# Chunked attention on one core: transposes by 32x32 blocks on VectorE, exchanged through DRAM

## The chip, the cores and the metric

The kernel runs on one core of one Trainium2 chip. The metric is the device time of one execution in microseconds (us); the median of three runs counts. "The profile" is one execution taken by the hardware profiler, and "the page" is its summary.

## What is computed

The reference applies four layers to x, 256 tokens of 1,024 channels, in float32: a gated delta rule, a causal attention of 8 heads, a retention of 4 heads, and a chunked attention of 16 heads of 128 dimensions. Only the last layer changes. Cut to what matters:

```
proj = h @ w_in                       # [256, 8192]
q, k, v, g = split(proj, 4)           # 16 heads of 128 each
q, k = rms_norm(q) * q_g, rms_norm(k) * k_g      # over the 128 of a head
s = q @ k.T / sqrt(128) + bias        # chunks of 64 tokens; what lies ahead of a chunk is masked
o = softmax(s) @ v * silu(g)
x = x + gate * (o @ w_out)            # the output of the kernel
```

## The kernel before

Weights come in units of 128x1024 float32 (512 KB), one DMA each on SyncE's queue into one of five `raw` buffers. ScalarE and VectorE split each unit exactly into two float32r parts, `whi` and `wlo` (`unit`, six pairs of buffers, `PARTS`); activations are kept in two parts as well (`hd_hi`, `hd_lo`), and a product is three products of parts. In layer d, the chunked attention, q, k and v come in quarters of four heads: `project_a` makes two PSUM banks of 128 tokens x 512 columns (two tiles of tokens) out of four units, 96 products of 512 columns. The gates g and the output come as 128 columns x 256 tokens out of one or two units, 24 products of 256 columns a unit (`project_b`).

A quarter of q or k is then normed (`normed`): ScalarE sums squares, GpSimd takes the power, VectorE multiplies PSUM by the factor into `xn` [128 tokens, 4 heads, 128], and four TensorE transposes against the identity (in the trace `con`) put it, head by head, into a PSUM bank. ScalarE copies the bank into `kr`, or reversed in its tokens and scaled into `qr`. A head (`head`, `attend`) waits for its quarters of q, k, v and its bias. Two float32 products give the scores, 384 columns: the first tile of queries with 128 keys, the second with 256. VectorE adds the bias and takes the least, ScalarE takes the exponential and its sum, VectorE divides. Three TensorE transposes turn the weights `s` around, ScalarE copies them from PSUM into `pT`, two products with `vr` give the output, and ScalarE copies that into one of five buffers `or`. A gate (`gate`) multiplies it by silu and splits it for the output projection; only then the buffer `or` comes free. `out_tile` makes 128 output channels at a time, adds them to xT and stores them.

The order of the instructions is written out by a small planner in the kernel (`Tasks`). Tasks are generators that yield operations; the planner gives each operation a time by estimates written in the code and issues per engine in the order in which the engines would take them by these estimates. On the chip each engine runs its instructions in that fixed order and waits on semaphores for the data. A DMA is estimated at 0.05 us and its bytes on the queue, and 2.0 us more until it has landed; a product in float32r at 0.42 ns a column. Priorities let heads go ahead of projections. PSUM has eight banks, in rings that change hands between layers; in layer d before: four for projections (`PJ`), one for scores (`SS`), one for the transposes of weights (`TT`), one for outputs (`OO`), one for the transposes of q and k (`MM`).

The order in which quarters come is a line of letters (line 157), and a head can start as soon as its q, k and v are done:

```
ORDER_D = "q1 k0 v0 q0 v2 g1 q2 k1 v1 q3 v3 g0 g3 k2 k3 g2".split()
```

Here "q1" is the quarter of heads 4 to 7, and the gates of heads 0 to 2 are made ahead, at the end of the layer before. The profile puts nearly all instructions on line 218, the helper that records them, so that groups are told apart by tile names.

Of the kernel before, what the change touches and what calls it, by code (L numbers as in the profile page):

```python
# [10 lines left out]
F32 = mybir.dt.float32  # L11
# [6 lines left out]
PSUM = bass.MemoryType.PSUM  # L18
# [8 lines left out]
# Per-partition columns: (name, number of columns)  # L27
# [12 lines left out]
# Constants that depend on shapes alone: (name, number of columns)  # L40
# [27 lines left out]
def _t5_hot():  # L68
    """[33, 384]: which bucket the relative position 255 - m falls in; the last row masks what lies ahead."""
    rel = 255 - np.arange(384)  # L70
    n = np.maximum(rel, 0)
    nf = np.maximum(n, 1).astype(np.float32)
    large = 16 + (np.log(nf / np.float32(16)) / np.float32(np.log(2048 / 16)) * np.float32(16)).astype(np.int32)
    bucket = np.where(n < 16, n, np.minimum(large, 31))
    hot = np.zeros((33, 384), np.float32)
    hot[bucket, np.arange(384)] = rel >= 0
    hot[32] = np.where(rel >= 0, 0.0, -1e30)
    return hot


def _decay():
    """[128 keys, 4 heads, 384]: key tile 0 with all queries, then key tile 1 with the last 128."""
# [29 lines left out]
def _plan():  # L112
    """The units of weights in the order of their use; those of the adaptive norms stand between the others."""
# [37 lines left out]
# Which units of weights are used whole, in float32 products  # L151
WHOLE = [("d_g", u) for u in (0,)] + [("a_qkv", u) for u in (0, 3, 4, 6, 7, 8, 9, 13, 14, 17, 18, 20, 22)]
# The order of the units
# [3 lines left out]
ORDER_D = "q1 k0 v0 q0 v2 g1 q2 k1 v1 q3 v3 g0 g3 k2 k3 g2".split()  # L157
ADA_FROM = ('a_z', 7)
ADA2_FROM = ('c_v', 3)
# Counts: units used before the norm, steps at once, units ahead, buffers  # L160
EARLY, BATCH, AHEAD, AHEAD2, FIRST_D, ADA_A, ADA2_EVERY = 1, 1, 1, 2, 3, 2, 1
RAWS, NPARTS, NKQ, NC, NVT = 5, 6, 3, 2, 2
# Priorities of tasks, the least goes first
# [4 lines left out]
# Estimates, in us  # L168
OVER, HOP, SAME = 0.03, 0.2, 0.1
DMA_LATENCY = 2.0  # L170
# [10 lines left out]
class Ring:  # L181
    """Free buffers: `b = yield ring` waits for one, ring.put(b) gives one back."""
# [22 lines left out]
class Engine:  # L205
    """Turns the calls of an engine into operations for a task to yield: (engine, estimated us, call, table)."""
# [57 lines left out]
def chain(*ops):  # L264
    """Operations of one engine, each on what the one before it made."""
    return [(e, c + SAME, f, t) for e, c, f, t in ops[:-1]] + [ops[-1]]


class Tasks:
    """Issues the instructions of concurrent tasks in the order in which the engines would take them.  # L270

    A task is a generator. It yields an operation or a list of operations of one engine, and goes on when they have
    ended by the estimates; a Ring, and gets a buffer; an Event, and waits for it; a number, its priority from there on
    (the least goes first)."""
# [59 lines left out]
    def dispatch(self, e):  # L334
# [18 lines left out]
        lat = DMA_LATENCY if e.startswith("D") else 0.0  # L353
# [5 lines left out]
        self.at(end + 1e-6, lambda: self.dispatch(e))  # the next operation of the same task may go first  # L359

    def hold(self, n):
        """While held, the vector and the scalar engine take nothing that can wait."""
        self.held += n
        if not self.held:
            for e in "VS":
                self.at(self.now, lambda e=e: self.dispatch(e))
# [10 lines left out]
def body(ctx, tc, a, out):  # L377
# [4 lines left out]
    dma, dma2 = Engine("D", nc.sync, _cost_dma), Engine("D2", nc.scalar, _cost_dma)  # L382

# [18 lines left out]
    con = tile_(keep, "con", [P, NCON])  # L402
# [9 lines left out]
    nc.scalar.activation(phalf, nhalf, AF.Copy, scale=-1.0)  # the activation table is loaded meanwhile  # L412

    # PSUM: rings of whole banks; they change hands between the layers
# [22 lines left out]
    def h_set(i, name, wide=0):  # L437
        """Two float32r parts of transposed activations."""
# [10 lines left out]
    # ------------------------------------------------------------ weights: units of [128, 1024], in the order of use  # L449
# [11 lines left out]
    def unit(u):  # L461
        """One unit, whole or split exactly into two float32r parts; what belongs to the adaptive norms is summed at once."""
        raw = yield RAW
        src = a[u[0]][u[1]]
        if number[u] == 0:  # its first half is used before the other is there
# [35 lines left out]
    def project_b(units, x, x32, ps, ready):  # L501
        """[128 columns, tokens] of a product. x: (hi, lo) of the transposed activations, x32: the same, not split."""
# [19 lines left out]
    def project_a(name, q, x, pss, ready):  # L522
        """Two [128 tokens, 512 columns] of a product, with four units."""
# [32 lines left out]
    def sums_ops(ps, srcs):  # L556
        """Sums over the partitions of [128, 256] each, tokens on partitions: [128 tokens, 2, 96]."""
# [3 lines left out]
    def row_ops(ps, c):  # L561
        """A pair of token columns along the free dimension, on every partition."""
# [6 lines left out]
    # ------------------------------------------------------------ gated delta rule  # L569
    def layer_a(pool):  # L570
# [44 lines left out]
        def load_consts():  # L615
            yield [dma.dma_start(out=wab, in_=a["a_ab"]), dma.dma_start(out=rows, in_=a["a_rows"].partition_broadcast(P)),
                   dma.dma_start(out=con[:, 2 * P:], in_=a["consts"][:, 2 * P:])] + [
# [9 lines left out]
        def x_square(i):  # L627
            """Squares of two column tiles, added to those before."""
# [30 lines left out]
        def decays():  # L659
            """gg = -exp(a_log) softplus(a + dt_bias), beta = sigmoid(b), tokens on partitions"""  # L660
# [34 lines left out]
        def decay(h):  # L695
            """decay[s, c] = exp(sum of gg over s < m <= c), where the products of queries and keys will stand"""
# [16 lines left out]
        def conv(ch, dst):  # L713
            """dst [128, 256] = silu(conv) of channel tile ch."""
# [36 lines left out]
        def squared(h, x, dst):  # L751
            """Sums of the squares of the columns of x [128, 256]."""
# [7 lines left out]
        def norm_k(h, kq, done):  # L760
            """nk = the norm of the keys, bb = beta / nk ** 2"""
# [14 lines left out]
        def head(h):  # L776
            """The system matrices of head h and its squared norms."""
# [13 lines left out]
            # k.k of key tile 0 (256) and 1 (128), q.k of key tile 0 (256) and 1 (128)  # L791
# [10 lines left out]
            # the 16 x 16 diagonal blocks, side by side; then only what lies between blocks stays in MT  # L802
# [10 lines left out]
        def base(q):  # L813
            """V16 = (I + U)^-1 for the strictly upper 16 x 16 problems of four heads, block rows on partitions."""
# [31 lines left out]
        def gates(q):  # L846
            """zs = silu(z)"""
# [8 lines left out]
        # block solves: (I + B)^-1 = D (I - F)(I + F^2)(I + F^4), F = N D  # L856
# [54 lines left out]
        def outputs(t, q):  # L911
            """The outputs of four heads on one tile of tokens, their norm and gate, transposed in two parts."""
# [68 lines left out]
    def out_a(o_in, z_in, box, after):  # L981
        """The rows of the first four heads for all columns, then those of the others, two column tiles at a time."""
# [7 lines left out]
        # the two column tiles of a bank are one group, begun with zeros  # L990
# [35 lines left out]
    # ------------------------------------------------------------ from one layer to the next  # L1026
    class Next:
        """What the end of a layer makes for the next: scaled activations and sums of squares, a column tile at a time."""
# [24 lines left out]
        def squares(self, n):  # L1053
            """Adds to the sum; works on pairs, but for the last."""
# [22 lines left out]
        def weighted_squares(self, n, w):  # L1077
            """Adds to sums over the channels, tokens on partitions, with one weight of two for each half of the columns."""
# [11 lines left out]
    def ahead(u, nx, box):  # L1090
        """A product begun before its layer is, before norm and shift; box[u] = PSUM, with the product of the shift behind it."""
# [15 lines left out]
    # ------------------------------------------------------------ softmax attention of one head  # L1107
    def attend(A, kT, qT, bias, vv, o, half):
        """o [128 dims, 256] = half times the output; queries stand reversed in their tile of 128 in qT and bias.

        x holds the negative scores, mx their least: minus the maximum of the scores."""
        ps = yield SS
        yield [pe.matmul(ps[:, :P], lhsT=qT[:, :P], rhs=kT[:, :P], start=True, stop=True),
               pe.matmul(ps[:, P:384], lhsT=qT[:, P:], rhs=kT, start=True, stop=True)]
# [11 lines left out]
        ps = yield TT  # L1126
        yield [pe.transpose(ps[:, i * P:(i + 1) * P], x[:, i * P:(i + 1) * P], ident) for i in range(3)]
        A["s"].put(item)
        pT = yield A["pT"]
        yield s.activation(pT, ps[:, :384], AF.Copy)  # L1130
        TT.put(ps)
        ps = yield OO
        yield [pe.matmul(ps[:, :T], lhsT=vv[0], rhs=pT[:, :T], start=True, stop=False),
               pe.matmul(ps[:, P:T], lhsT=vv[1], rhs=pT[:, T:], start=False, stop=True)]
# [10 lines left out]
    def gate_out(o, zs, hi, lo):  # L1145
        """The two parts of o * zs."""
# [4 lines left out]
    # ------------------------------------------------------------ MoBA (one block of 256: causal attention within it)  # L1151
    def layer_b(pool, nx, begun, after):
# [16 lines left out]
        def biases():  # L1169
            """Rows of rel = 255 .. -127 for each head, then [128 - 1 - query, key]."""  # L1170
# [79 lines left out]
        def head(h):  # L1250
# [3 lines left out]
            yield from attend(A, K[h], Q[h], b_bias[:, h], [VV[q][:, t, hh * P:(hh + 1) * P] for t in range(2)], O[h], 1.0)  # L1254
# [43 lines left out]
    # ------------------------------------------------------------ adaptive norms  # L1298
    def cond(condb):
        """condb: silu(c) along the free dimension, on every partition"""  # L1300
# [4 lines left out]
    def ada(i, nx):  # L1305
        """mods[i] [128, 24]: shift, 1 + scale and gate of layer i as columns"""
# [11 lines left out]
    def modulate(hs, i, nx, k, r12, Y, r_in, done):  # L1318
        """hs = parts of rms_norm(x) * norm_g * (1 + scale) + shift"""
# [566 lines left out]
```

## Time and profile before

| what | value |
|---|---|
| three runs, us | 806.8, 804.44, 802.66; median 804.44 |
| span of the profiled execution, first to last instruction | 799.7 us |
| what lies around that span, against the median | 4.7 us |
| TensorE busy in the span | 787.7 us, 98% |
| VectorE, ScalarE, GpSimd busy | 566.3, 456.7, 37.6 us |
| first product of layer d on `hd_hi` | 546.3 us |
| last output product of a head of layer d | 755.7 us |

An engine's busy time counts its instructions from start to end. TensorE's products are pipelined: they start every 0.12 to 0.23 us though each lasts longer, so that the distance between starts says more than the mean of one.

### The profile page before, as it was taken

Reading aid. Unit: us, or ns where it says so; the run is one execution under the profiler, and the core shown is the slowest. Engines: PE = TensorE matmul, PEld = TensorE weight load, DVE = VectorE, ACT = ScalarE, POOL = GpSimd, SP = SyncE. Lnnn points to the kernel's source line nnn. Section 1 sums busy time; section 2 is a strip of 40 time slices with the busy share of each in tenths; the row PEclk is TensorE's granted clock in tenths of the full one; section 3 lists DMA queues with packets and bytes.
Section 4 is the critical chain, followed back from the end, with each engine's and each line's share of the span. In section 5 each row is a group of like instructions: output and inputs, shape, how many; then the busy total and the mean of one; then the engine's idle time right before and its main releaser. Section 6 shows DMA issues by size and latency. Waiting matters only on the chain.

```text
span 799.7 us, 13581 instructions
## 1 busy us (share of the span) xinstructions
PE 787.7 (98%) x5117; PEld 710.3 (89%) x5117; DVE 566.3 (71%) x1157; ACT 456.7 (57%) x968; POOL 37.6 (5%) x45
## 2 busy tenths in 40 slices
PE   6999999999999999999999999999999999999998
PEld 5898889989899999998888879998889888989998
DVE  5799998346997978698467889768547556557751
ACT  4886453545635786644445454655657567558740
POOL 0120100010000000000000000000100000000000
PEclk9999999999999999999999999999999999999999
DMA  8536443125768866728558899865654665564340
GB/s 286 181 106 210 133 143 120 55 80 174 254 219 324 296 218 203 239 77 286 158 142 275 304 309 325 259 185 191 211 177 128 209 181 151 171 187 132 103 132 27
DMA packets 45946, 151.15 MB, mean 189 GB/s; under 512 B 5135, under 2 KB 10040, under 8 KB 45880
## 3 DMA queue, kind: packets, MB, share of 16 engines
q1 hardware_dynamic: 44824, 149.22, 57.9%
q10 hardware_dynamic: 1056, 1.06, 0.5%
q8 instruction: 40, 0.66, 0.3%
q14 instruction: 26, 0.21, 0.1%
HBM read 149.20 MB, written 1.06 MB: 188 GB/s over the span
## 4 chain that ended last, share of the span: by engine, by line
PE 98%; DMA 1%; DVE 0%; ACT 0%; issue 0%; POOL 0%; SPq 0%; DVEq 0%
PE bank L218 98%; DMA xT<-in_xT 1%; ACT js L218 0%; POOL rs L218 0%; DVE r L218 0%; DVE hi L218 0%; ACT r L218 0%; DVE xT L218 0%; DVE lo L218 0%; ACT rsrow L218 0%; SPq L218 0%; DVE rs L218 0%; ACT whi L218 0%; DVEq L218 0%
## 5 line engine op out<-in xcount | busy, mean ns | idle before, releaser
L218 ACT ACTIVATE whi<-raw 128x1024 fp32r<-128x1024 f32 x210 | 222.2, 1060 | 200.8 <-PE bank L218 168.5
L218 DVE TENSOR_TENSOR wlo<-raw,whi 128x1024 fp32r<-128x1024 f32 x210 | 256.0, 1223 | 104.9 <-ACT whi L218 103.8
L218 PE MATMUL bank<-whi,hd_hi 128*128 128x512 f32 x192 | 78.0, 406 | 0.0
L218 PE MATMUL bank<-wlo,hd_hi 128*128 128x512 f32 x192 | 75.7, 394 | 0.0
L218 PE MATMUL bank<-whi,hd_lo 128*128 128x512 f32 x192 | 75.6, 394 | 0.0
L218 DVE CUSTOM_DVE_ANT_0 raw<-raw,condb 128x1024 f32<-128x1024 f32 x48 | 58.5, 1220 | 8.9 <-DMA raw<-in_ada 8.8
L218 PE MATMUL bank<-whi,hc_hi 128*128 128x512 f32 x128 | 52.0, 406 | 0.0
L218 PE MATMUL bank<-whi,hc_lo 128*128 128x512 f32 x128 | 50.5, 395 | 0.0
L218 PE MATMUL bank<-wlo,hc_hi 128*128 128x512 f32 x128 | 50.4, 394 | 0.0
L218 PE MATMUL bank<-lo,raw 128*128 128x256 f32 x192 | 44.3, 379 | 0.9 <-DVE lo L218 0.9
L218 PEld LDWEIGHTS bank<-whi,hd_lo 128*128 128x128 f32 x192 | 36.2, 188 | 8.6
L218 PEld LDWEIGHTS bank<-whi,hd_hi 128*128 128x128 f32 x192 | 36.1, 188 | 7.4
L218 PEld LDWEIGHTS bank<-wlo,hd_hi 128*128 128x128 f32 x192 | 36.2, 188 | 7.4
L218 PEld LDWEIGHTS bank<-lo,raw 128*128 128x128 f32 x192 | 35.1, 189 | 5.4 <-DVE lo L218 1.1
L218 PE MATMUL bank<-hb_hi,whi 128*128 128x256 f32 x128 | 38.4, 300 | 0.0
L218 PE MATMUL bank<-hb_hi,wlo 128*128 128x256 f32 x128 | 36.3, 283 | 0.0
L218 PE MATMUL bank<-hb_lo,whi 128*128 128x256 f32 x128 | 36.1, 282 | 0.0
L218 PE MATMUL bank<-hd_hi,whi 128*128 128x256 f32 x104 | 31.7, 305 | 0.0
L218 PE MATMUL bank<-ha_hi,whi 128*128 128x256 f32 (+1 forms) x96 | 29.5, 307 | 0.0
L218 PE MATMUL bank<-hd_hi,wlo 128*128 128x256 f32 x104 | 29.3, 282 | 0.0
L218 PE MATMUL bank<-hd_lo,whi 128*128 128x256 f32 x104 | 29.3, 282 | 0.0
L218 PEld LDWEIGHTS bank<-whi,hc_lo 128*128 128x128 f32 x128 | 24.1, 188 | 5.7
(322 smaller groups left out, 2157.3 us busy)
## 6 DMA issues: line engine op xcount, KB each, us to landing
raw<-in_ada SPq DMA_DIRECT2D x48, 512.0 KB, 4.6
raw<-in_a_qkv SPq DMA_DIRECT2D x23, 512.0 KB, 4.6
raw<-in_c_v SPq DMA_DIRECT2D x16, 512.0 KB, 4.3
raw<-in_c_g SPq DMA_DIRECT2D x16, 512.0 KB, 4.0
raw<-in_c_out SPq DMA_DIRECT2D x16, 512.0 KB, 4.9
raw<-in_d_g SPq DMA_DIRECT2D x16, 512.0 KB, 3.7
raw<-in_d_q SPq DMA_DIRECT2D x16, 512.0 KB, 3.6
raw<-in_d_k SPq DMA_DIRECT2D x16, 512.0 KB, 3.6
```

The lines of the kernel that those rows point to most:

```text
L218: return self.key, c, lambda: f(*a, **k), func and func.name
```

## The change

In layer d TensorE transposes nothing any more. VectorE transposes each 32x32 block in its place and writes the blocks in an order by which those that belong together lie side by side in a row (`blocks`, `z`). The tile goes out to DRAM in one DMA (`turn_out`), and four DMAs (`turn_in`), each for 32 partitions, read it back so that the row of blocks becomes a column of blocks: with the transposed blocks that is the whole transpose. For a quarter of q or k (128x1024) a piece of these reads is 1,024 bytes long, for a head's weights (128x384) 384 bytes. The reads go into `kr` and `pT` directly; for q they go into a buffer first, from which ScalarE makes `qr`. These DMAs are issued on SyncE's queue, with the weights, and the planner has its own estimate for them: 0.45 us each on the queue and 4.0 us more. Operands of scores and output products are read in runs of 32 elements, because blocks stay interleaved.

Buffers: `z` for q and k is the tile of the silu of c, used no more; a second one and two for the weights come out of the tile x32 as soon as the layer's own activations are made (`more`); a buffer for q is where the constants of the first layer were. The bank of `MM` goes to `PJ`, that of `TT` to `SS`. The quarters come in another order. The other attention (layer b) keeps its transposes on TensorE. Elsewhere the diff takes out comments alone; its core:

```diff
-ORDER_D = "q1 k0 v0 q0 v2 g1 q2 k1 v1 q3 v3 g0 g3 k2 k3 g2".split()
+ORDER_D = "q1 k1 q0 v1 k0 v0 q2 g1 k2 v2 q3 k3 g0 v3 g2 g3".split()
...
-DMA_LATENCY = 2.0
+LATENCY = {"D": 2.0, "D2": 2.0, "DB": 4.0}
...
+    swap = Engine("DB", nc.sync, lambda *x: 0.45)
...
-    con = tile_(keep, "con", [P, NCON])
+    con = tile_(keep, "con", [P, 10 * P])
...
+    def turn_out(z, d):
+        return swap.dma_start(out=d, in_=z)
+    def turn_in(dst, d):
+        w = dst.shape[1] // 4
+        return [swap.dma_start(out=dst[32 * b:32 * b + 32].rearrange("j (a c) -> j a c", c=w),
+                               in_=bass.AP(tensor=d.tensor, offset=d.offset + b * w, ap=[[4 * w, 32], [128 * w, 4], [1, w]]))
+                for b in range(4)]
+    def blocks(x, n):
+        return x.rearrange("p (a m i) -> p m a i", a=4, m=n)
     def attend(A, kT, qT, bias, vv, o, half):
-
-        x holds the negative scores, mx their least: minus the maximum of the scores."""
         ps = yield SS
-        yield [pe.matmul(ps[:, :P], lhsT=qT[:, :P], rhs=kT[:, :P], start=True, stop=True),
-               pe.matmul(ps[:, P:384], lhsT=qT[:, P:], rhs=kT, start=True, stop=True)]
+        yield [pe.matmul(ps[:, :P].rearrange("p (a i) -> p a i", a=4), lhsT=qT[:, 0], rhs=kT[:, 0], start=True, stop=True),
+               pe.matmul(ps[:, P:384].rearrange("p (t a i) -> p t a i", t=2, a=4), lhsT=qT[:, 1], rhs=kT, start=True, stop=True)]
...
-        ps = yield TT
-        yield [pe.transpose(ps[:, i * P:(i + 1) * P], x[:, i * P:(i + 1) * P], ident) for i in range(3)]
-        A["s"].put(item)
-        pT = yield A["pT"]
-        yield s.activation(pT, ps[:, :384], AF.Copy)
-        TT.put(ps)
+        if "z" not in A:
+            ps = yield TT
+            yield [pe.transpose(ps[:, i * P:(i + 1) * P], x[:, i * P:(i + 1) * P], ident) for i in range(3)]
+            A["s"].put(item)
+            pT = yield A["pT"]
+            yield s.activation(pT, ps[:, :384], AF.Copy)
+            TT.put(ps)
+        else:
+            z = yield A["z"]
+            yield v.transpose(blocks(z, 3), x.rearrange("p (m b i) -> p m b i", m=3, b=4))
+            A["s"].put(item)
+            d = tc.dram_tile([P, 384], F32, name="p_d")
+            yield turn_out(z, d)
+            A["z"].put(z)
+            pT = yield A["pT"]
+            yield turn_in(pT, d)
         ps = yield OO
-        yield [pe.matmul(ps[:, :T], lhsT=vv[0], rhs=pT[:, :T], start=True, stop=False),
-               pe.matmul(ps[:, P:T], lhsT=vv[1], rhs=pT[:, T:], start=False, stop=True)]
+        x = blocks(pT, 3) if "z" in A else pT.rearrange("p (m a i) -> p m a i", m=3, a=4)
+        o2 = ps[:, :T].rearrange("p (m a i) -> p m a i", m=2, a=4)
+        yield [pe.matmul(o2, lhsT=vv[0], rhs=x[:, :2], start=True, stop=False),
+               pe.matmul(o2[:, 1], lhsT=vv[1], rhs=x[:, 2], start=False, stop=True)]
...
-        m, rs, r12, qkg = buf("m", [P, 2]), buf("rs", [P, 2]), buf("r12", [P, T]), buf("qkg", [P, 1])
+        A["z"] = Ring(run, [])
+        m, rs, r12, qkg = buf("m", [P, 2]), buf("rs", [P, 2]), acc[:, 0], buf("qkg", [P, 1])
+        ZX, QT = Ring(run, [late["condb"]]), Ring(run, [con[:, 2 * P:]])
         hs = h_set(0, "hd")
         oT = sixteen(pool, "od", nx.hs)
         Y, XN, FR = Ring(run, [r.free[0][:, i] for r in SQ for i in range(2)]), ring(pool, "xn", [P, 4, P], 3), Ring(run, [(buf(f"ms{i}", [P, 2, 4]), buf(f"fr{i}", [P, 2, 4])) for i in range(2)])
-        QR, KR, VR = (ring(pool, n, [P, 4, 2, P], 2) for n in ("qr", "kr", "vr"))
+        QR, KR, VR = (ring(pool, n, x, 2) for n, x in (("qr", [P, 1024]), ("kr", [P, 1024]), ("vr", [P, 4, 2, P])))
...
-            MM.put(ps)
+            PJ.put(ps)
...
-                ps = yield MM
-                yield [pe.transpose(ps[:, hh * P:(hh + 1) * P], xn[:, hh], ident) for hh in range(4)]
+                if t == 0:
+                    z = yield ZX
+                yield v.transpose(blocks(z, 8)[:, 4 * t:4 * t + 4], xn.rearrange("p h (b i) -> p h b i", b=4))
                 XN.put(xn)
-                x = ps.rearrange("p (h i) -> p h i", h=4)
-                if reverse:
-                    yield qkg_in
-                    yield s.activation(dst[:, :, t, ::-1], x, AF.Copy, scale=qkg)
-                else:
-                    yield s.activation(dst[:, :, t], x, AF.Copy)
-                MM.put(ps)
+            d = tc.dram_tile([P, 1024], F32, name=name + "_d")
+            yield turn_out(z, d)
+            ZX.put(z)
+            if reverse:
+                x = yield QT
+                yield turn_in(x, d)
+                yield qkg_in
+                for t in range(2):
+                    yield s.activation(dst[:, t * 512:(t + 1) * 512].rearrange("p (h a i) -> p h a i", h=4, a=4),
+                                       blocks(x, 8)[:, 4 * t:4 * t + 4, ::-1, ::-1], AF.Copy, scale=qkg)
+                QT.put(x)
+            else:
+                yield turn_in(dst, d)
...
-            yield from attend(A, K[q][:, hh].rearrange("p t i -> p (t i)"), Q[q][:, hh].rearrange("p t i -> p (t i)"),
+            yield from attend(A, blocks(K[q], 8)[:, hh::4], Q[q].rearrange("p (t h i) -> p t h i", t=2, h=4)[:, :, hh],
                               B[q][:, hh], [VV[q][:, hh, t] for t in range(2)], o, 0.5)
...
+        def more():
+            for e in hs_in + [first["in", ("d_g", u)] for u in range(FIRST_D)]:
+                yield e
+            x = x32_tile("zd", 2).rearrange("p k t -> p (k t)")
+            for i in range(2):
+                A["z"].put(x[:, 1024 + i * 384:1024 + (i + 1) * 384])
+            ZX.put(x[:, :1024])
+        run.spawn(more(), 1)
...
-        yield from hand_over(OO, TT)
+        yield from hand_over(OO, SS)
```

## Rows read from the trace of the kernel before

**Rows 1.** The page's head: busy time, share of the span, instructions.

```profile
span 799.7 us, 13581 instructions
PE 787.7 (98%) x5117; PEld 710.3 (89%) x5117; DVE 566.3 (71%) x1157; ACT 456.7 (57%) x968; POOL 37.6 (5%) x45
```

**Rows 2.** The chain that ended last, longest piece: start, us, what.

```profile
171.91 624.54 PE bank L218 x4079
```

**Rows 3.** TensorE's groups, 546 to 760 us: busy us, mean ns.

```profile
L218 PE MATMUL bank<-con,xn 128*128 128x128 f32 x64 | 9.6, 273 | 0.0
...
L218 PE MATMUL bank<-con,s 128*128 128x128 f32 x48 | 7.9, 273 | 0.0
```

**Rows 4.** TensorE's timeline at two groups of transposes: start us, us.

```profile
564.58 0.39 PE L218 MATMUL bank<-wlo,hd_hi 128*128 128x512 f32 x1
564.81 0.40 PE L218 MATMUL bank<-whi,hd_lo 128*128 128x512 f32 x1
565.05 0.60 PE L218 MATMUL bank<-con,xn 128*128 128x128 f32 x4
565.41 0.48 PE L218 MATMUL bank<-whi,hd_hi 128*128 128x512 f32 x1
565.73 0.39 PE L218 MATMUL bank<-wlo,hd_hi 128*128 128x512 f32 x1
...
754.20 0.28 PE L218 MATMUL bank<-xd_hi,wlo 128*128 128x256 f32 x1
754.32 0.49 PE L218 MATMUL bank<-con,s 128*128 128x128 f32 x3
754.57 0.36 PE L218 MATMUL bank<-xd_hi,whi 128*128 128x256 f32 x1
754.77 0.28 PE L218 MATMUL bank<-xd_lo,whi 128*128 128x256 f32 x1
754.89 0.28 PE L218 MATMUL bank<-xd_hi,wlo 128*128 128x256 f32 x1
```

**Rows 5.** VectorE's and ScalarE's groups, 546 to 760 us: busy us, mean ns.

```profile
L218 DVE TENSOR_TENSOR wlo<-raw,whi 128x1024 fp32r<-128x1024 f32 x64 | 78.2, 1225 | 61.6 <-ACT whi L218 60.8 <-PE bank L218 0.7
L218 DVE TENSOR_TENSOR xn<-bank,fr 128x512 f32<-128x512 f32 x16 | 10.9, 683 | 0.2 <-POOL fr L218 0.2
...
L218 ACT ACTIVATE pT<-bank 128x384 f32<-128x384 f32 x16 | 7.8, 489 | 1.2 <-PE bank L218 1.1
...
L218 ACT ACTIVATE kr<-bank 128x512 f32<-128x512 f32 x8 | 4.8, 598 | 6.6 <-PE bank L218 6.6
```

**Rows 6.** Stretch of eight heads: busy us of PE, PEld, DVE, ACT, POOL; clock, DMA.

```profile
724.00:757.00 33.00, 33.00 (x254) 31.91 (x253) 24.93 (x85) 26.61 (x84) 1.64 (x1) 1.00 0.35 104
```

**Rows 7.** SyncE's DMA issues, timeline: start us, us of the issue.

```profile
538.12 0.33 SPq L218 DMA_DIRECT2D raw<-in_d_k  x1
538.54 0.39 SPq L218 DMA_DIRECT2D br<-in_d_rel  x1
```

**Rows 8.** SyncE's waits, 546 to 757 us: total us, times, longest.

```profile
SPq L218 <- DVE wlo L218: 132.0, 49, 9.9
```

**Rows 9.** Timeline: the first d_out load, the first d_out product.

```profile
709.83 0.33 SPq L218 DMA_DIRECT2D raw<-in_d_out  x1
...
756.29 0.48 PE L218 MATMUL bank<-od,whi 128*128 128x256 f32 x2
```

**Rows 10.** Issue to landing: eight xT stores of 128 KB; weights from 546 us.

```profile
L218 SPq DMA_DIRECT2D out<-xT x8: 332/338/425, 760.3 to 797.0; - x8
...
DMA to landing us min/median/max: 1.9/2.9/4.7
...
DMA to landing us min/median/max: 3.4/3.6/5.5
```

**Rows 11.** DMA queues: packets, MB, share; 546 to 760 us, then whole span.

```profile
q1 hardware_dynamic: 10272, 34.61, 53.8%
...
q10 hardware_dynamic: 1056, 1.06, 0.5%
```

More of the change, by code (lines that the diff above doesn't have):

```diff
@@ L352, in dispatch @@
         self.free[e] = end
-        lat = DMA_LATENCY if e.startswith("D") else 0.0
+        lat = LATENCY.get(e, 0.0)
         def ended():
@@ L616, in load_consts @@
             yield [dma.dma_start(out=wab, in_=a["a_ab"]), dma.dma_start(out=rows, in_=a["a_rows"].partition_broadcast(P)),
-                   dma.dma_start(out=con[:, 2 * P:], in_=a["consts"][:, 2 * P:])] + [
+                   dma.dma_start(out=con[:, 2 * P:NCON], in_=a["consts"][:, 2 * P:])] + [
                 dma.dma_start(out=V16[q], in_=a["blk_id"]) for q in range(2)]
@@ L1253, in head @@
                 yield e
-            yield from attend(A, K[h], Q[h], b_bias[:, h], [VV[q][:, t, hh * P:(hh + 1) * P] for t in range(2)], O[h], 1.0)
+            yield from attend(A, K[h].rearrange("p (t a i) -> p t a i", t=2, a=4), Q[h].rearrange("p (t i) -> p t i", t=2), b_bias[:, h], [VV[q][:, t, hh * P:(hh + 1) * P] for t in range(2)], O[h], 1.0)
             run.set(o_in[h])
```

## The prediction

> **What bounds the kernel now.** I read the head of the page first. TensorE is busy 98% of the span; the other engines are not near it [rows 1]. A busy TensorE can still hide gaps, so the chain of waits came next: from 171.9 us to the last product, 624.5 us on end, it is TensorE behind TensorE, with no other engine in between [rows 2]. The changed layer (from about 546 us to the end) lies wholly inside. So in this layer one us of TensorE work taken away is one us of time, if what replaces it is never late; and one us for which TensorE waits, its queue being in order, is one us of time, too. Work put on VectorE, ScalarE, SyncE or the DMA engines costs nothing as long as it isn't late.
>
> **What is taken from TensorE.** The changed layer has 64 transposes of xn (16 groups of four: q and k, four quarters, two token tiles) and 48 of s (16 groups of three, one a head) [rows 3]. The row "mean of one", 273 ns, is no price: it is the length of a pipelined instruction. The price is how much later the next products start. One product of 512 columns follows the other in 0.23 us. From the last one ahead of the group of four at 564.81 to the second one behind it at 565.73 are 0.92 us, where two steps without transposes are 0.46: the group costs 0.46 us, the slower restart behind it included [rows 4]. For the group of three: 754.20 to 754.77 are 0.57 us, two steps of 0.12 are 0.24, cost 0.33 us [rows 4]. The sum: 16 x 0.46 + 16 x 0.33 = 7.4 + 5.3 = 12.6 us. Scores and outputs of the heads stay as many and as large. Their operands are read in runs of 32 elements now; no row shows what that costs, the row of the contiguous form gives nothing, and I take nothing; were it a restart of each, it would be at most the 0.1 us by which a product is later behind a group (565.73 - 565.41 = 0.32 against 0.23), twice a head: 32 x 0.1 = 3 us.
>
> **What is moved to VectorE and ScalarE.** VectorE gets 16 transposes of 128x512 and 16 of 128x384. The trace has none of either; the nearest rows are 683 ns for 128x512 with an operand in PSUM and 1225 ns for 128x1024, so 0.6 to 0.7 us for the first; for the second 0.46 (three eighths of 1225) to 0.68 [rows 5]. I take 0.65 and 0.5: 16 x 0.65 + 16 x 0.5 = 18.4 us. ScalarE loses the copies into kr (8 x 0.598) and pT (16 x 0.489), 12.6 us, and keeps those into qr [rows 5]. Where heads stand closest, eight of them between 724 and 757 us, VectorE is busy 24.9 of 33 us [rows 6]; eight more transposes of 0.5 make it 28.9. So VectorE still fits, and the cost on the path is 0. Were it full there, 0.5 us a head would come on top, 16 x 0.5 = 8 us.
>
> **What the exchange costs.** A head's weights go out as one DMA of 192 KB and come back as four of 48 KB, pieces of 384 bytes; a q or k quarter goes out as 512 KB and comes back as four of 128 KB, pieces of 1,024 bytes. That is 24 x 5 = 120 DMAs more on SyncE's queue, 0.33 to 0.39 us each to issue [rows 7]: 40 to 47 us of a queue that between 546 and 757 us waits 132 us for VectorE to free weight buffers [rows 8]. It has room; what it queues is the next weights, and those are far ahead: the first of d_out is issued at 709.8 us and used at 756.3 [rows 9]. So late weights cost 0 unless SyncE lags by tens of us.
>
> The trip itself stands between softmax and output product. Bounds: a 128 KB write lands in 1.9 us at best, 2.9 in the median, a 512 KB load in 3.4 to 5.5 [rows 10]. So out 1.9 to 5.5, three further issues 1.0 to 1.2, the last read 1.9 to 5.5: 4.8 to 12.2 us. I take 3.2 + 1.1 + 3.3 = 7.6, since bytes and crowding lie between the two median rows. The kernel's own plan, which fixes TensorE's order, allows 0.45 + 4.0 out and 4 x 0.45 + 4.0 in: 10.25 us. So at my price data are there 2.6 us before TensorE's turn, and at the upper end 2.0 us after. What covers the trip is projections: after heads 4 to 7 come k0 and v0, after 0 to 3 q2 and g1, after 8 to 11 q3 and k3, after 12 to 15 g2 and g3. Each letter is four units, 4 x 12 x 0.23 = 11 us. Without this cover a trip a group of four heads would be 4 x 7.6 = 30 us. For q and k, the value quarter or another one stands between the projection and its heads, again 11 us or more, so their eight trips are hidden. The reordering does only that: it costs no TensorE work. I add 0.25 us a group (one issue that stands ahead in SyncE's queue is 0.33), 1.0 us.
>
> A weak point is the four reads. The rows show that one queue has several DMAs under way: two issues at 538.12 and 538.54 us, each landing only us later [rows 7, 10], so four reads should overlap. The Trainium skill, "DMA: Bandwidth & Descriptors", section "Rules for kernel authors", speaks against the change: small transfers should be made one large one, as under 64 KB overhead is most of the cost. By the rows' overlap the trip is 7.6 us; by that rule taken as one overhead after the other it becomes the second rival below.
>
> **Sum.** 799.7 us of span [rows 1] - 12.6 + 1.0 = 788.1; the median of the runs shown, 804.44, lies 4.7 us above that span, so the forecast is 792.8 us, 1.4% faster. What a measurement here can tell from no change is about 0.5%, 4 us.
>
> **Rivals.**
> 1. *Trips late by a little.* At the upper bound each group of heads holds TensorE for 2.0 us, 8 us in all: 791.8 + 8 = 799.8 us. For it: DMA engines are 53.8% busy in the layer, and the trips add to that [rows 11]. A packet of 1 KB took 0.5% x 16 x 799.7 / 1056 = 0.06 us; 24 x 512 such pieces and the writes by their bytes (7.3 MB at 53.8% x 16 x 214 / 34.6 = 53 us per MB) are (745 + 390) / 16 = 71 us of all engines in some 200. So it would be near 90% with the longest assumption for the 384-byte pieces. Against it: weights come early and don't press.
> 2. *The four reads of a head one after another.* 3.2 + 4 x 2.9 [rows 10] = 14.8 us, 4.6 late, four groups: 18.2 us, so 791.8 + 18.2 = 810.0 us, slower. It decides from 12.6 / 4 = 3.2 us late a group. Against it: the overlap of issues above. By the page's fixed cost of about 2.0 us a DMA (same page, "Anatomy of one DMA") four reads would be an estimated 8 us and the time about 796; no run so far shows it.
> 3. *The last heads.* Only five output buffers (OR) are there; while heads 8 to 11 wait for their gates in g2, heads 13 to 15 get a buffer only as those gates finish. If head 15's trip begins as late as the end of g3, what covers it is the first d_out tile, 15 steps of three products, 15 x 3 x 0.12 = 5.4 us: TensorE waits 2.2 (trip 7.6) to 6.8 us (12.2), about 4.5: 796.3 us. For it: each gate needs its own unit of 24 x 0.12 = 2.9 us. Against it: g2 and g3 are 23 us long.
> 4. *Weights late.* If SyncE, held by waits for trips, loses the lead of 46 us [rows 9], TensorE waits for weights. The DMA sum above says 90% at most, so a lag of some 10 us would be needed to eat the gain: 802 to 808 us.
>
> **Chances.** Forecast 0.62; first rival 0.13 (0.08 of it over 0.5% faster, 0.05 within); second 0.09, slower; third 0.11, faster; fourth 0.05 (0.03 within, 0.02 slower). Faster 0.62 + 0.08 + 0.11 = 0.81, same 0.08, slower 0.11. The range: from no wait at all, 791.8, less the 1.8 us by which the fastest run lies under the median, 790.0, to the first rival with about 1 us of that spread, 801. It leaves out the second rival and most of the fourth, about 0.14, and a little at either end. The likeliest case alone: 790 to 795.
>
> **What would show it.** Right: transposes of xn gone from TensorE, those of s down to 24 (the other attention's); 32 VectorE transposes of 0.5 to 0.7 us; TensorE's steps in the layer still without a gap; last product near 784.8 us. A trip from VectorE's transpose to the output product's first possible start under 10 us. The first rival: TensorE's waits list DMA into pT, some 2 us a group; the second: the same, over 3 us, and reads that land one by one; the third: one gap of 2 to 7 us between the last gate unit and the first d_out products' end; the fourth: ScalarE's splits wait for weights. Wrong would be the price of the groups if steps between products grew where no wait is shown: then strided operands cost.

## The result

The changed kernel takes 794.35 us (median of 4 runs, 791.45 to 798.13), the kernel before 803.62 us beside it (802.66 to 806.8): a ratio of 0.9884, 95% interval [0.9846, 0.9922]. Forecast were 792.8 us, 790.0 to 801.0. In a second set of runs it was 794.73 us against 802.49, 0.990 [0.9882, 0.9919].

The profiled execution has a span of 792.6 us and a time of 794.41. The head of its page, which answers to [rows 1]:

```profile
span 792.6 us, 13576 instructions
PE 777.4 (98%) x5005; PEld 700.5 (88%) x5005; DVE 581.7 (73%) x1189; ACT 444.4 (56%) x944; POOL 37.4 (5%) x45
```

112 TensorE instructions are gone, VectorE's busy time rose by 15 us, ScalarE's fell by 12. The groups by tile names show what stands in their place: the transposes of the heads (min, median, max in ns), those of the k quarters (the eight of the q quarters, 0.71 us each too, go into `condb`), and what is left of TensorE's transposes of s, all before 294 us and so of the other attention:

```profile
L218 DVE STREAM_TRANSPOSE zd<-s x16: 558/573/579, 599.1 to 736.4; 128x384 f32<-128x384 f32 x16
L218 DVE STREAM_TRANSPOSE zd<-xn x8: 703/705/711, 577.5 to 704.3; 128x512 f32<-128x512 f32 x8
...
L218 PE MATMUL bank<-con,s x24: 270/272/274, 259.6 to 293.2; 128*128 128x128 f32 x24
```

The chain of waits is no longer one piece. TensorE's waits from 540 us on (total, times, longest) are one line, and the chain of waits leads it back through a read and a write of the k3 quarter (start, us, what):

```profile
PE bank L218 <- DMA kr<-d_k_d: 2.5, 1, 2.5
```

```profile
706.06 8.21 DMA d_k_d<-zd
...
715.65 3.73 DMA kr<-d_k_d
719.38 0.14 issue
719.52 69.71 PE bank L218 x557
```

VectorE had finished that quarter at 705.0 us. SyncE issued the write at 706.06, behind four reads of q3 and a load of weights; it landed 8.2 us later, the four reads took 1.3 us to issue, and the last one 3.7 to land. With the 1.05 us ahead of the write that is 14.4 us, where the planner allows 10.25. TensorE's timeline there shows what it cost:

```profile
716.75 0.28 PE L218 MATMUL bank<-hd_hi,wlo 128*128 128x256 f32 x1
719.52 0.89 PE L218 MATMUL bank<-kr,qr 128*128 128x128 f32 x4 [2.48 <-DMA kr<-d_k_d]
720.06 0.47 PE L218 MATMUL bank<-hd_hi,whi 128*128 128x256 f32 x1
720.36 0.28 PE L218 MATMUL bank<-hd_lo,whi 128*128 128x256 f32 x1
720.48 0.33 PE L218 MATMUL bank<-hd_hi,wlo 128*128 128x256 f32 x1
720.61 0.41 PE L218 MATMUL bank<-hd_hi,whi 128*128 128x256 f32 x1
720.82 0.41 PE L218 MATMUL bank<-hd_lo,whi 128*128 128x256 f32 x1
```

From 716.75 to 719.52 are 2.77 us instead of one step of 0.12: 2.65 us lost. Then the steps of 256 columns are 0.21 us, not 0.12. That is the clock; the stretches (columns: length, then busy time and count of PE, PEld, DVE, ACT and POOL, then the granted clock as a share of 2.4 GHz, the DMA engines' share and GB/s):

```profile
720.00:721.50 1.50, 1.50 (x10) 1.45 (x10) 1.05 (x6) 0.72 (x3) 0.00 (x0) 0.69 1.01 391
721.50:723.00 1.50, 1.50 (x9) 1.50 (x9) 1.50 (x3) 0.69 (x3) 0.00 (x0) 0.50 0.37 150
723.00:724.50 1.50, 1.50 (x10) 1.48 (x9) 0.30 (x2) 0.00 (x0) 0.00 (x0) 0.67 0.48 49
724.50:726.00 1.50, 1.50 (x15) 1.47 (x14) 1.25 (x7) 0.96 (x1) 0.00 (x0) 1.00 0.62 240
```

So from about 720.5 us, one us after it started again, to about 724 TensorE works at 1.2 GHz. Fifteen steps there take 3.20 us instead of 1.79, and the two groups of scores 0.07 and 0.09 more: 1.6 us. In sum, the layer's products run from 547.3 to 788.9 us, 241.6 us, where before they ran from 546.3 to 796.15, 249.9 us. 12.6 - 2.65 - 1.6 = 8.35 against the 8.26 that this is shorter.

The DMA queue between 546 and 760 us answers to the first line of [rows 11]:

```profile
q1 hardware_dynamic: 28223, 50.62, 77.3%
```

That mean hides the stretch that counts here. While the write of k3 was under way the DMA engines were full (their share is the last column but one):

```profile
700.00:705.00 5.00, 5.00 (x24) 4.15 (x23) 4.11 (x7) 2.27 (x3) 0.00 (x0) 1.00 1.10 321
705.00:710.00 5.00, 5.00 (x25) 4.18 (x25) 1.88 (x3) 2.07 (x4) 0.00 (x0) 1.00 0.94 226
710.00:715.00 5.00, 5.00 (x41) 4.82 (x40) 1.92 (x3) 4.46 (x7) 0.00 (x0) 1.00 0.68 273
```

The 0.68 is an average of full engines up to about 713 us and nearly idle ones behind it, when the write was through and its reads were still to be issued.

### The profile page after: what moved, and what is told of

It reads as the page before. It is cut to its first block, busy times and chain, and to the rows that moved or that the text cites. A ratio compares the mean times of both kernels' runs of the same rounds, so it can differ in the third digit from the quotient of the medians.

```text
span 792.6 us, 13576 instructions
## 1 busy us (share of the span) xinstructions
PE 777.4 (98%) x5005; PEld 700.5 (88%) x5005; DVE 581.7 (73%) x1189; ACT 444.4 (56%) x944; POOL 37.4 (5%) x45
## 4 chain that ended last, share of the span: by engine, by line
PE 94%; DMA 3%; DVE 1%; ACT 1%; issue 1%; SPq 0%; POOL 0%; DVEq 0%; ACTq 0%
PE bank L218 94%; DMA d_k_d<-zd 1%; DMA raw<-in_d_g 1%; DMA raw<-in_a_z 1%; DMA xT<-in_xT 1%; DMA kr<-d_k_d 0%; SPq L218 0%; ACT xn L218 0%; DVE wlo L218 0%; ACT js L218 0%; POOL rs L218 0%; DVE r L218 0%; ACT sq L218 0%; DVE hi L218 0%; ACT r L218 0%
## 5 line engine op out<-in xcount | busy, mean ns | idle before, releaser
L218 PE MATMUL bank<-hb_hi,wlo 128*128 128x256 f32 x128 | 36.2, 283 | 0.0
```

Source lines behind the costliest of these rows:

```text
L218: return self.key, c, lambda: f(*a, **k), func and func.name
```

## The experiments

"Saved" is always against runs of the kernel before on the same chip. Waits are those of TensorE in the changed layer, in the profiled execution.

**No exchange.** VectorE's transposes and the interleaved operands stay; the DMAs between them are gone. The cut shows the heads; q and k are changed likewise.

```diff
-            z = yield A["z"]
-            yield v.transpose(blocks(z, 3), x.rearrange("p (m b i) -> p m b i", m=3, b=4))
+            pT = yield A["pT"]
+            yield v.transpose(blocks(pT, 3), x.rearrange("p (m b i) -> p m b i", m=3, b=4))
...
-            yield turn_out(z, d)
-            A["z"].put(z)
-            pT = yield A["pT"]
-            yield turn_in(pT, d)
```

> This kernel leaves the exchange through DRAM out: VectorE writes its 32x32 blocks straight into the operands, so q, k and the weights of the heads are only transposed within blocks. Theory A (the 12.6 us of transposes come off TensorE in full, and what is missing, 4.3 us in the profile of the changed kernel, is one wait for the k3 quarter's trip with the low clock behind it): no wait of TensorE in the layer, 803.6 - 12.6 = 791.0 us. Theory B (operands in runs of 32 elements, or VectorE's added work, cost the rest): no trip, but still about 794 us.

789.91 us against 802.65, ratio 0.9835 [0.9811, 0.9858]: 12.7 us saved, no wait in the layer. So the price of the transposes, 12.6 us, is right to 0.1 us, and neither VectorE's 20 us of transposes (16 x 0.57 + 16 x 0.71) nor the operands in runs of 32 take time beside it: theory B falls.

**Heads only.** q and k are transposed on TensorE again, as before; the weights of the heads go through DRAM.

> Only the weights of the heads go by VectorE and DRAM; q and k are transposed on TensorE as before; new order of the quarters. Theory A: 16 x 0.33 = 5.3 us saved and no wait, 798.3 us. Rival (the trips of the heads are late, 48 KB reads one after another): TensorE waits for DMA into pT, over 3 us in a group of heads, 800 us or more.

797.11 us against 802.65, 0.9927 [0.99, 0.9955]: 5.5 us saved, where 16 x 0.33 is 5.3. In the layer TensorE never waits for a head's trip. Its 48 KB reads land as follows:

```profile
DMA to landing us min/median/max: 1.8/4.0/5.3
```

The Trainium skill's rule against small transfers ("DMA: Bandwidth & Descriptors", "Rules for kernel authors") thus holds for what a read costs, 4.0 us for 48 KB where 512 KB of weights took 3.6 to 4.2 in the same run; but as four are under way together and TensorE has projections to do meanwhile, it costs no time.

**Quarters only.** The weights of the heads stay on TensorE, q and k go through DRAM.

> Only q and k go by VectorE and DRAM; the weights of the heads are transposed on TensorE as before; new order of the quarters. Theory A: 16 x 0.46 = 7.4 us saved, 796.2 us, less what a late k quarter costs: with a wait as in the changed kernel 796.2 + 4.3 = 800.5; without the heads' traffic the DMA engines are freer and the wait is shorter, so 796 to 800, and a wait for DMA into kr if there is one. Theory B: no wait, and under 7.4 us saved.

798.69 us against 802.65, 0.9953 [0.9939, 0.9967]: 4.0 us saved of 7.4. TensorE's waits, and the reads of the k quarters:

```profile
PE bank L218 <- DMA kr<-d_k_d: 4.2, 3, 1.7
```

```profile
DMA to landing us min/median/max: 2.8/6.6/7.5
```

7.4 - 4.2 = 3.2. So these waits belong to the k quarters, not to the heads, and they are there without the heads' traffic. The granted clock stays at 1.00 through these three.

**A longer estimate for q and k in the planner.**

```diff
-LATENCY = {"D": 2.0, "D2": 2.0, "DB": 4.0}
+LATENCY = {"D": 2.0, "D2": 2.0, "DB": 4.0, "DQ": 9.0}
...
-        return swap.dma_start(out=d, in_=z)
+        return (swap if z.shape[1] == 384 else swapq).dma_start(out=d, in_=z)
```

Here `swapq` is the engine "DQ", which is SyncE's queue too. Only the write of a quarter is on it; its four reads keep the old estimate.

> The changed kernel, with a longer estimate in the planner for the trips of q and k alone (9.0 us instead of 4.0 to land), so that it puts the heads of k3 later in TensorE's order. Theory A: the wait for DMA into kr is gone, 791.0 us, some 3 us under the changed kernel. Theory C (the DMA engines are so crowded that something else is late instead): another wait turns up, about 794 us.

799.18 us against 802.65, 0.9957 [0.9942, 0.9972]: worse than the changed kernel, and than either theory had it. TensorE's waits in the layer:

```profile
PE bank L218 <- ACT whi L218: 2.8, 1, 2.8
PE bank L218 <- DMA pT<-p_d: 2.7, 3, 1.2
PE bank L218 <- DMA kr<-d_k_d: 1.6, 1, 1.6
PE bank L218 <- ACT vr L218: 1.3, 1, 1.3
```

8.4 us in sum, 12.6 - 8.4 = 4.2 against 3.5 saved. The wait of 2.8 us is put down to ScalarE, but it stands ahead of a head's output products at 721.47 us (`bank<-pT,vr`), and a read of that head's weights landed at 721.23: it is a late trip as well. Theory A in its narrow form, one late trip that a longer allowance mends, falls: the heads of k3 wait no more, but the allowance moves all that follows in the order, and other trips are late in the new one; the reads of k land in 5.1 to 9.0 us there. That fits theory C but does not show it by itself, since the longer estimate also lengthens trips: it puts the reads later in SyncE's own order. Those of k2 are issued 10.9 us after their write (682.89 and 671.95 us), behind four loads of weights; in the changed kernel it is 5.7 us (674.06 and 668.40). The wait of 2.8 us leaves the granted clock at 1.00.

**Half of the weight bytes.** Each weight DMA of the last layer brings the first half of its unit; the planner still counts it as the whole.

```diff
-        yield dma.dma_start(out=raw, in_=src)
+        if u[0][:2] == "d_":
+            e, c, f, t = dma.dma_start(out=raw, in_=src)
+            yield e, c, dma.dma_start(out=raw[:, :512], in_=src[:, :512])[2], t
+        else:
+            yield dma.dma_start(out=raw, in_=src)
```

> The changed kernel, in which the weight DMAs of the last layer bring only the first half of each unit (the other half of the buffer keeps older weights, so the layer's output is not the reference's); the instructions, the planner's estimates and every wait are otherwise the same. Theory C (the trip of a k quarter is late because its DMAs share the DMA engines with the weights): with half the weight bytes the wait for DMA into kr is gone, 791 us, and the last read of a k quarter lands in under 4 us. Rival D (the trip is late by itself, 1 KB pieces of DRAM that was just written): wait as in the changed kernel, 794 us.

789.52 us against 802.42, 0.9833 [0.981, 0.9856]: 12.9 us saved and no wait, with all 120 DMAs of the exchange in place. The queue from 546 to 760 us, then the landings of the k reads:

```profile
q1 hardware_dynamic: 28560, 33.96, 53.7%
```

```profile
DMA to landing us min/median/max: 2.4/3.3/4.1
```

Rival D falls: the same pieces of the same DRAM are in time as soon as less else is moved, which is theory C. The write of k3 is issued at 704.48 us and its reads at 709.45, 5.0 us later instead of 8.3. At a share of 54%, that of the kernel before, the k reads land in 3.3 us in the median, which is what I had taken for a read. The mean share alone doesn't order the runs, though: the median is 3.9 us in the changed kernel at 77%, 6.6 with the quarters alone at 70%, and 3.2 at 74% in the run with the old order below. The Trainium skill ("DMA: Bandwidth & Descriptors", "Latency and other measured facts") gives HBM's access latency as 0.2 us on average and 2 us at high load. The runs agree with the direction: weights of the layer landed in 3.6 us in the median before, in 4.4 to 5.4 us in the changed kernel; whether HBM or the sharing of the DMA engines makes the difference they don't tell.

**The exchange on GpSimd's queue.**

```diff
-    swap = Engine("DB", nc.sync, lambda *x: 0.45)
+    swap = Engine("DB", nc.gpsimd, lambda *x: 0.45)
```

> The changed kernel with the 120 DMAs of the exchange issued on GpSimd's queue, no longer behind the weights on SyncE's. If the order on SyncE's queue makes the k quarter late (its write was issued 1.1 us after VectorE was done with it, and reads go behind whole weight units), the wait shrinks or goes, 791 to 793 us. If the DMA engines themselves are crowded, no better, 794 us; if GpSimd takes longer to issue a DMA than SyncE's 0.33 to 0.43 us, other trips become late and the time goes over 797 us.

810.05 us against 802.42, 1.0094 [1.0063, 1.0126]: slower than the kernel before by 0.9%. TensorE waits 9.8 us for pT (7 times) and 5.4 for kr (2 times). GpSimd's timeline shows a reason: it works in order, the powers of the norms among the DMAs, and issues a read in 0.55 us, where SyncE takes 0.42:

```profile
587.10 2.18 POOL L218 DMA_DIRECT2D kr<-d_k_d  x4 [6.13 <-DMA d_k_d<-zd]
589.30 2.22 POOL L218 TENSOR_TENSOR fr<-ms,nhalf 128x8 f32<-128x8 f32 x1
595.74 0.60 POOL L218 DMA_DIRECT2D d_q_d<-condb  x1 [4.22 <-DVE condb L218]
601.96 2.19 POOL L218 DMA_DIRECT2D con<-d_q_d  x4 [5.62 <-DMA d_q_d<-condb]
604.14 1.11 POOL L218 DMA_DIRECT2D p_d<-zd  x2
```

VectorE had the weights of two heads ready at 600.6 and 601.7 us, but their writes went out from 604.14 on, because GpSimd stood 5.6 us for the write of q and then issued q's four reads. The reads of kr land in 5.0 us in the median, no sooner than in the changed kernel (3.9). So the move to a queue without the weights didn't help here. What SyncE's order costs by itself this run doesn't show, since GpSimd's queue is of another kind (`software_dynamic` in the page) and slower to issue; of the trip of k3 in the first profile, 1.05 of 14.4 us were spent in that order.

**The old order with the exchange, and the new order without it.**

```diff
-ORDER_D = "q1 k1 q0 v1 k0 v0 q2 g1 k2 v2 q3 k3 g0 v3 g2 g3".split()
+ORDER_D = "q1 k0 v0 q0 v2 g1 q2 k1 v1 q3 v3 g0 g3 k2 k3 g2".split()
```

> The changed kernel with the old order of the quarters. What the new order is for by the prediction: cover for the trips. In the old order k3 is the last but one letter, so the trip of k3 and those of heads 12 to 15 have only g2 (11 us) to hide under: some 10 to 20 us uncovered, 799 to 806 us. If the order did not matter: 794 us.

> The kernel before, with nothing but the new order of the quarters; all transposes stay on TensorE. By the prediction the order moves no work and only gives cover: same as before, 802.5 us, within 0.3%, and no wait of TensorE in the layer. If the order were part of the gain: 797 to 800 us.

The changed kernel in the old order: 819.98 us against 802.42, 1.0215 [1.0179, 1.025]. The kernel before in the new order: 803.39 against 802.49, 1.0007 [0.9997, 1.0016]. So the order is worth nothing by itself, and 25 us to the exchange. That is more than I expected. TensorE's waits in the old order:

```profile
PE bank L218 <- DMA pT<-p_d: 10.7, 3, 5.4
PE bank L218 <- DVE zr L218: 4.6, 2, 2.6
PE bank L218 <- DMA kr<-d_k_d: 2.8, 1, 2.8
```

With 2.5 us of smaller ones they are 20.6 us, and the mean granted clock of the span is 0.987, worth 0.013 x 818 = 10.6 us: 12.6 - 20.6 - 10.6 = -18.6, measured -17.6.

**g2 ahead of v3.** This puts the products of g2, 11 us, between k3 and the heads that read it.

```diff
-ORDER_D = "q1 k1 q0 v1 k0 v0 q2 g1 k2 v2 q3 k3 g0 v3 g2 g3".split()
+ORDER_D = "q1 k1 q0 v1 k0 v0 q2 g1 k2 v2 q3 k3 g0 g2 v3 g3".split()
```

> The changed kernel with g2 moved ahead of v3, so that 11 us more lie between the projection of k3 and the heads that read it, and 11 us less behind those heads. Theory C with the trip of k3 the only late one: the wait for DMA into kr is gone, 791 us, if g3 and the first d_out tiles cover the last heads. Otherwise a wait for DMA into pT or for the last heads' outputs at the end, 794 to 800 us.

> The changed kernel again, to stand beside its variants on one chip. 794.35 us in its first runs, with runs from 791.45 to 798.13: if the wait for a k quarter comes and goes with the crowding of the DMA engines, this spread of several us is there again, and the profile shows at least one wait of TensorE for DMA into kr or pT.

> The variant with g2 ahead of v3 again, in more rounds: 791 to 792 us, 2 to 3 us under the changed kernel of the same call, waits of TensorE in the layer under 1 us in sum.

791.95 us, 0.9863 [0.9834, 0.9892]; in the second set of runs 791.33 us, 0.9861 [0.9843, 0.9879], where the changed kernel of the same set has 0.990 [0.9882, 0.9919]. The intervals do not overlap, if barely; this is the fastest complete kernel here. In its first profile the heads of k3 start at 725.5 us, 20.4 us after VectorE's last transpose of k3, where the changed kernel starts them 14.5 us after it, its wait included. Its only wait in the layer in the second profile, and then those of the changed kernel beside it:

```profile
PE bank L218 <- DMA kr<-d_k_d: 0.3, 1, 0.3
```

```profile
PE bank L218 <- DMA kr<-d_k_d: 3.3, 3, 2.1
PE bank L218 <- DMA pT<-p_d: 0.9, 1, 0.9
```

The changed kernel's waits are not the same ones in each execution: one of 2.5 us in the first profile, four of 4.2 us in this one. That is where its spread of 5 to 7 us between runs can come from; it was not followed run by run.

**The reads of a head issued twice.**

```diff
+    def twice(dst, d):
+        return [(e, 0.0, f, t) for e, c, f, t in turn_in(dst, d)] + turn_in(dst, d)
...
-            yield turn_in(pT, d)
+            yield twice(pT, d)
```

> The changed kernel, with the four reads of a head's weights issued twice over (the same bytes to the same place), while the planner allows the time of one set. This adds some 1.7 us of issues and 512 pieces of 384 bytes to each of the 16 trips. The first trip of the changed kernel is ready some 1 to 2 us before TensorE's turn, so if the heads' margin is that thin, TensorE now waits for DMA into pT in each of four groups, 1 to 3 us each: 797 to 804 us. If the margin were the 2.6 us of the prediction or more, under 2 us lost: 794 to 796 us.

838.74 us against 802.49, 1.0448 [1.0432, 1.0464], far past what I expected. I had overlooked that the second set writes what the first one writes, so that it waits until the first has landed: SyncE's waits say so (33.0 us in 15 waits for DMA into pT). So each trip is longer by a whole read and not by its issues, and the trips behind it wait in SyncE's order: from VectorE's transpose to the last landing that the trace shows they take 8.3 to 24.4 us, where those of the changed kernel take 6.2 to 14.0. The run became a test of what trips cost that are much too late. TensorE's waits in the layer:

```profile
PE bank L218 <- DMA pT<-p_d: 31.3, 10, 6.1
PE bank L218 <- DMA kr<-d_k_d: 2.6, 2, 1.7
```

33.9 us of waits and a mean granted clock of 0.982 (0.018 x 838 = 15 us): 12.6 - 33.9 - 15 = -36.3, and 36.2 us were lost.

## Why the prediction was right, point by point

- *TensorE is the bound, a us for a us.* Right. Over the runs, what is saved is what TensorE has less to do less its waits less the low clock, within about 1 us (2.4 in the run on GpSimd's queue with its 11 waits; a wait costs somewhat more than its length, in the first profile 2.65 us for 2.48): 12.7 and 12.9 where there is no wait, 11.2 (the sum gives 12.6 - 0.3 = 12.3) for g2 ahead of v3, 7.8 (12.6 - 4.2 = 8.4) for the changed kernel in the second set. Part of what is left over lies ahead of the layer, whose first product comes between 546.1 and 548.0 us in the profiles.
- *0.46 and 0.33 us a group, 12.6 us.* Right, as a sum and in its two parts: 5.5 for the heads, against 5.3; the quarters' 7.4 by the difference of the runs without a wait, 12.7 - 5.5 = 7.2.
- *VectorE's transposes.* 0.57 us for 128x384 and 0.71 for 128x512, taken as 0.5 and 0.65; the first within its bounds, the second a hair above them. Both are off the path, as is the rest of VectorE's, ScalarE's and GpSimd's work.
- *A head's trip.* Its size was wrong, its price about right. A write landed in 3.4 us and a read in 4.1 in the medians, taken as 3.2 and 3.3. But the sum of 7.6 us left out, but for 0.25 us a group, the time for which a trip waits its turn in SyncE's order. From the end of VectorE's transpose to the last landing that the trace shows, the trips of the first profile take 6.2 to 14.0 us, 11 in the median, and ten of the 16 take over 10 us, the bound set under "What would show it". A trip longer than the plan's 10.25 us need not hold TensorE up, then, as the prediction reckoned it would: in the first profile no head made TensorE wait, in the second one did, for 0.9 us, after a trip of 14.9. The 1.0 us of waits was put in the wrong place. How thin the margin is shows in the eighth head of the first profile. VectorE's transpose ends at 654.30 us, the write is the second of the two from 653.08 on, the reads are issued from 660.66 on, and the last landing shown, at 667.12, comes 0.16 us ahead of TensorE:

```profile
653.73 0.57 DVE L218 STREAM_TRANSPOSE zd<-s 128x384 f32<-128x384 f32 x1
653.08 1.57 SPq L218 DMA_DIRECT2D p_d<-zd  x2
660.66 3.54 SPq L218 DMA_DIRECT2D pT<-p_d  x4
667.28 0.83 PE L218 MATMUL bank<-pT,vr 128*128 128x256 f32 x4
```

- *"So their eight trips are hidden".* This step failed. I took the bounds of a landing from a layer whose DMA engines are 53.8% busy, and said myself that they would be near 90%, without letting that lengthen the trips of 512 KB. At 77% the write of k3 took 8.2 us (upper bound: 5.5), and reads of k took up to 7.5 in the run of the quarters alone, at 70%. What is lost is one wait of 2.5 us in the first profile, 4.25 with the restart and the low clock behind it, and four waits of 4.2 us together in the second. It is the same mechanism as the first rival's, in another place.
- *The price of a wait.* I counted a wait as its length. In the first profile 2.65 us of standstill brought 1.6 us of low clock behind it.
- *Second rival.* Its four waits, one a group, were too few. The run with the reads twice has ten waits for 16 heads, and lost 44 us against the changed kernel; its trips, up to 24.4 us, are longer than the rival's 14.8, so what the rival itself would have cost is not shown. It did not come true because the reads of a head overlap (48 KB reads land in 4.1 us in the median, the four are issued within 1.3 to 1.4 us where SyncE isn't held up).
- *Third rival and fourth.* The last heads did not hold TensorE up, and no weights were late: neither has a line in TensorE's waits in the changed kernel.
- *Span and time.* What lies around the span was 1.8 us in the runs that give both, not 4.7: the kernel before was profiled in one of its faster executions. The forecast of 788.1 us of span fell 4.5 us short for that run: the wait and the clock cost 4.25 us where 1.0 was set aside, and the layer also began 1.0 us later than before (547.3 against 546.3). The 2.9 us too much around the span made up for most of it, so that the time was only 1.6 us off. That closeness is luck: 11.6 us were forecast to be saved (804.44 - 792.8), and 9.3 were, 7.8 in the second set.

## What to carry to other kernels

On a kernel that one engine bounds, price a removed operation by the distance of the starts of its neighbours with and without it; that held here to 0.3 us. Work that is moved to DMA is free only against the landings of the crowded queue, not of the queue before: add the new traffic, and give transfers of half a MB several us more than the rows of before show, and count the time in which a DMA waits its turn on the engine that issues it. When an order of instructions is fixed by estimates, a longer estimate makes another order, with late trips of its own; here more work between the start of a trip and its use mended what a longer estimate, for the write alone, did not.

## What was not expected of the hardware

- After a standstill of 2.5 us TensorE's granted clock was 0.50 for some us (steps of 0.21 us for 256 columns); waits of 1.0 to 1.7 us in the run of the quarters alone and one of 2.8 us in the run with the longer estimate left it at 1.00. What decides between the two stays open.
- A TensorE product whose moving operand lies in runs of 32 elements, 384 or 1,024 bytes apart, starts the next one no later than a contiguous one: a group of four scores or four outputs costs 0.65 to 0.67 us before and after (from the last product ahead of the group to the second one behind it 0.89 us among products of 256 columns and 1.12 among those of 512, less two steps).
